# Expert gates built eight tokens at a time, on VectorE alone

## The chip, the cores and the metric

The kernel runs on one core of one Trainium2 chip. The metric is the device time of one execution in microseconds; lower is better. All times below are of that core.

## The reference, cut to what matters

A two-layer network over 256 latent tokens and 256 context tokens, 1024 features wide. Each layer has a mixer (gMLP in layer 0, S5 in layer 1) and then a PEER expert network: each token picks, in each of 8 heads, 16 of 128 x 128 = 16384 experts by a product of two keys, and adds up `gate * gelu(h . u) * v` over the 128 picked experts.

```python
s = einsum("nhkd,hkmd->nhkm", q, sub_keys)         # scores of both key halves
s_half, i_half = top_k(s, 16)
cand = s_half[:, :, 0, :, None] + s_half[:, :, 1, None, :]
top_s, top_c = top_k(cand.reshape(128, 8, 256), 16)
k1 = take(i_half[:, :, 0], top_c // 16); k2 = take(i_half[:, :, 1], top_c % 16)
ids = k1 * 128 + k2
g = softmax(top_s)
act = gelu(einsum("nd,nhkd->nhk", h, u_tab[ids]))
out = einsum("nhk,nhkd->nd", g * act, v_tab[ids])
```

## The kernel before

**Dense experts.** For the first 384 tokens of layer 0 and all 256 latents of layer 1 the kernel doesn't gather rows. It multiplies the tokens with all 16384 experts, in 128 chunks of 128 (`k1` is the chunk, `k2` the row in it), and weights each activation with a gate that is zero where the token didn't pick the expert. `dense` has two halves. In the first, `front(k1)` for the first chunks (62 of 64 in layer 0, 66 of 68 in layer 1, then the last two) loads 512 KB of `peer_ut`, splits it into a high and a low part (`uh` by ScalarE at L296, `ul` by VectorE and GpSimd in turn at L298: one of three by VectorE in layer 0, one of two in layer 1), multiplies on TensorE (24 products, L304 to L306), applies GELU (L708) and puts the result into DRAM. After each of these chunks `during(k1)` moves the other work of the stage on by an even share of its steps. In the second half `back(k1)` reads the gates back (`Gr`), weights the activations and multiplies with `peer_v`.

**The other work of the first half** is a chain written in `layer0` (L1351) and `layer1` (L1422): `route` of a block of 128 tokens (top-16 searches on VectorE), then the next block's `route` in turn with the first block's `gate_units`, and so on; the last block's `gate_units` runs alone. Layer 0 has three blocks, layer 1 two. `between()` drains this chain, and the last two `front`s are issued behind the last gate product (`issue_after(ends["gates"])`, L751), so the second half starts behind it.

**`gate_units`** (L626) builds the table `gd[group, k2, k1, token]`. Keys and gates of the block are transposed, so that the 128 picks lie on partitions and the tokens along the row. For four tokens (`R = 4`) it makes one-hot rows: `o2` marks the pick's `k2` (L664, VectorE), `eq` its `k1` (L666, VectorE); `o1` holds `eq` times the gate's high part (L668, VectorE) and low part (L669: GpSimd, but VectorE for the third block of layer 0). All are float16. `iot`, the numbers 0 to 127 each written four times, is made once at the start (L457). In the tiles the token is the innermost index, so the product of token m reads its operands at a step of four elements, 8 bytes:

```python
nc.tensor.matmul(o, o2[:, :, m], o1[:, 0, :, m], start=True, stop=False)
nc.tensor.matmul(o, o2[:, :, m], o1[:, 1, :, m], start=False, stop=True)
```

There are eight such products (L653, L654) for four tokens; ScalarE copies the sum out of the bank (L655), and every 16 tokens go to DRAM. The products lag two steps behind the one-hot rows (`pend`), and `o2`, `eq` and `o1` have four buffers each. Each block has 32 such units; layer 0 has 96, layer 1 has 64.

**Order.** The work is written in program order, and a planner then orders the instructions of each engine by its own estimate of when each can run. Each engine executes its own list in that order. Only TensorE's order in the second half of `dense` and in S5 is as written.

Of the kernel before, what the change touches and what calls it, by code (L numbers as in the profile page):

```python
# [107 lines left out]
HG = 0  # L108


@with_exitstack
def tile_hybrid(ctx: ExitStack, tc: tile.TileContext, I, out, stop=None):
# [11 lines left out]
    def urgent(n):  # L124
        """A context of instructions that go before others."""
        return tc.high_priority(n) if n else ExitStack()
# [46 lines left out]
    def scale_cols(i, f, nf):  # L173
        """Norm gain times (1 + scale), for the blocks f..f+nf if they are a scale's."""
        for a, n, s in ((A1, i, 8), (A2, 2 + i, 32)):
            if s <= f < s + 8:
                b = slice(f - s, f - s + nf)
                nc.vector.tensor_scalar(a[:, i, b], mod[:, i, f:f + nf, :], 1.0, None, op0=OP.add)
                nc.vector.tensor_tensor(a[:, i, b], a[:, i, b],
                                        ng[:, n, b].unsqueeze(2).to_broadcast([P, nf, 2]), op=OP.mult)  # L180

    def ada_pe(pa, f):
        """Shift, scale and gate of the first mixer on the tensor engine: rows, transposed to columns."""
# [22 lines left out]
    def ada_rows(pa, blocks, cB=None, e=nc.vector):  # L206
        """The other modulations as row products, a block of 128 features at a time, on engine e."""
# [29 lines left out]
    def rsqrt(v, r, y):  # L237
        """r = 1 / sqrt(v): a first value from the exponent's bits, refined by Newton steps."""
# [8 lines left out]
    def norm_add(pl, pm, b, t0, t1, e=nc.gpsimd):  # L247
        """Add block b's squares of the columns t0..t1: all but the last blocks' in a tile, then over the
        features, to the first columns of pm, with tokens on partitions."""
# [14 lines left out]
    def norm_end(pl, pm, n, r=None):  # L264
        """1 / sqrt(mean of squares + eps) on every partition; computed with tokens on partitions."""
# [26 lines left out]
    def split(hi, lo, src, dve=1, gps=1):  # L292
        """src (float32) as hi + lo, exactly, both in the format of one-pass products; the lower
        part by DVE and GpSimd in turn, in the given proportion."""
# [5 lines left out]
    def mm3(o, pairs):  # L300
        """o = sum over pairs of lhsT^T rhs, each operand (hi, lo); lo times lo is below float32's rounding."""
# [7 lines left out]
    def modulate(pl, r, i, a, sh, parts, keep=None):  # L309
        """The normalised, modulated columns of XT as hi + lo, for parts (c, t0, t1, hi, lo); r from column parts[0].t0."""  # L310
# [14 lines left out]
    def residual(src, i, b, gate, part, view=lambda x: x):  # L325
        """XT block b += gate * src (columns as in XT)."""
# [8 lines left out]
    def gmlp(gw, hh, hl, r, vpump, vdone, upump, mid, pump):  # L335
        """Adds the mixer's output to XT; r = the norm of the result's columns."""
# [4 lines left out]
        with ExitStack() as st:  # L341
# [42 lines left out]
            def spatial(h):  # L384
# [10 lines left out]
                # the parts take the places of values that are no longer needed  # L395
# [16 lines left out]
            # the norm's gain and shift pass through the spatial product: gain * product + (shift * row sums + b_s)  # L412
# [43 lines left out]
    iot = cp.tile([P, KEYS, 4], F16, name="iot")  # L456
    nc.vector.tensor_copy(iot, i128.unsqueeze(2).to_broadcast([P, KEYS, 4]))  # L457
# [8 lines left out]
    def route(pr, S, gates, ids, kk, big={}):  # L466
        """Gates, both halves' keys and expert ids [P, heads, TOPK] from the scores [P, heads, 2, KEYS]."""
# [46 lines left out]
    # The score of a key is h . (w_q . key): the products of w_q with the keys come first.  # L514
    wp_d = [[dr.tile([P, KB, 512], F32, name=f"wp{i}_{q}") for q in range(4)] for i in range(2)]

    def wprime_units(pw, i, nb, e):
        """wp_d[i][pair of heads][d, block, (head, half, key)]; each step makes the products of one (head, half).
        e: the second engine of the copies."""
# [29 lines left out]
    def score_weights(i, pw, lo=(1, 2)):  # L549
        """The weights of scores, head by head, as (hi, lo)."""  # L550
# [9 lines left out]
    def scores(weights, ahead, pieces, S, done=lambda q: None):  # L560
        """S[block][token, head, half, key] from the pieces (hi, lo) of 128 tokens; ahead = weights already made."""
# [9 lines left out]
    def add_back(i, acc, a0, m, p0=0):  # L571
        """XT columns a0..a0+m += gate * acc, acc of [token, feature] from row p0."""
# [9 lines left out]
    # Experts of a token one by one: their rows are gathered.  # L582
    def gather_units(pg, i, hn, gates, ids, nh, finish, step=2):
        """Rows of the experts ids[:, head, slot], for nh heads; yields after `step` gathers; finish(acc)."""
# [35 lines left out]
    # All experts for the first n tokens: U^T chunks, GELU, gates (zero where an expert was not chosen), V chunks.  # L620
# [5 lines left out]
    def gate_units(pg, i, gates, kk, nt, g0, second):  # L626
        """gd[group, k2, k1, token] = the sum of the gates of expert (k1, k2), for nt tokens of a block. A gate
        is the sum of two float16, scaled by a power of two; places in a row are one-hot."""
        R = 4
        tr = pg.tile([P, 3, P], F32, name="jT", bufs=1)  # L630
# [3 lines left out]
        nc.scalar.copy(tr.rearrange("p q n -> p (q n)"), pm[:, 0:3 * P])  # L634
        kt = pg.tile([P, 2, P], F16, name="kt16", bufs=1)
        nc.vector.tensor_copy(kt, tr[:, 0:2])
        gt = pg.tile([P, 2, P], F16, name="gt16", bufs=1)
        gs = pg.tile([P, P], F32, name="gs", bufs=1)
        nc.vector.tensor_scalar(gs, tr[:, 2], GSCALE, None, op0=OP.mult)
# [3 lines left out]
        sh = [P, KEYS, R]  # L643
        pend = []

        def products(u, o1, o2):
# [4 lines left out]
            for m in range(R):  # L651
                o = pm[:, m * P:(m + 1) * P]
                nc.tensor.matmul(o, o2[:, :, m], o1[:, 0, :, m], start=True, stop=False)  # L653
                ends["gates"] = nc.tensor.matmul(o, o2[:, :, m], o1[:, 1, :, m], start=False, stop=True).ins  # L654
# [6 lines left out]
        for u in range(nt // R):  # L661
            ns = slice(u * R, u * R + R)
            o2 = pg.tile(sh, F16, name="o2", bufs=4)
            nc.vector.tensor_tensor(o2, iot, kt[:, 1, ns].unsqueeze(1).to_broadcast(sh), op=OP.is_equal)  # L664
            eq = pg.tile(sh, F16, name="eq", bufs=4)
            nc.vector.tensor_tensor(eq, iot, kt[:, 0, ns].unsqueeze(1).to_broadcast(sh), op=OP.is_equal)  # L666
            o1 = pg.tile([P, 2] + sh[1:], F16, name="o1", bufs=4)
            one = nc.vector.tensor_tensor(o1[:, 0], eq, gt[:, 0, ns].unsqueeze(1).to_broadcast(sh), op=OP.mult)  # L668
            second.tensor_tensor(o1[:, 1], eq, gt[:, 1, ns].unsqueeze(1).to_broadcast(sh), op=OP.mult)  # L669
            ends["places"] = one.ins  # L670
            pend.append((u, o1, o2))
            if len(pend) > 2:
                products(*pend.pop(0))
            yield
# [5 lines left out]
    def dense(pd, back_pool, i, n, hh, hl, ahead, keep, abanks, vbanks, during, between, pump,  # L680
              dve=(0, 1), vdve=(1, 1), finish=None):
        """The products of the first n tokens with all experts. The first `ahead` chunks' activations come
        before between(), all but the last `keep` of them put into DRAM."""
# [4 lines left out]
        def gate_rows(blk, g0, g1):  # L688
            """The gates of kg chunks, groups of tokens g0..g1."""
# [111 lines left out]
    def s5_setup(pp, sm):  # L801
        """The S5 mixer's powers and input coefficients; partitions are (direction, state)."""
# [56 lines left out]
        # powers of a in the order of a chunk's places, the second direction running backward  # L859
# [12 lines left out]
    def phase_units(pw):  # L872
        """ph_d[group, k] = (rot[0] + i rot[1]) ** k, where rho (rot[0] + i rot[1]) = a^L; the skip's gains added
        to the kernels' diagonals."""
# [677 lines left out]
```

## Time and profile before

| | |
|---|---|
| runs | 3183.05, 3179.83, 3183.05 us; median 3183.05 |
| span of the profiled execution | 3178.6 us (its first to its last instruction; 4.45 us below the median of the runs) |
| TensorE busy, mean granted clock | 2783.3 us, 88%; 0.935 |
| VectorE busy | 2500.6 us, 79% |
| ScalarE busy | 1325.5 us, 42% |
| GpSimd busy | 1777.4 us, 56% |
| all DMA | 738.94 MB, 232 GB/s over the span |

A busy share is a mean over stages with different limits. A TensorE interval includes its way through the array, and following ones overlap, so TensorE's throughput is read from the distance between starts. The granted clock is a share of full speed.

### The profile page before, as it was taken

The page shows a single profiled execution, that of the slowest core. Times are in us where ns is not written, and L with a number is a line of the kernel's source. Part 1 is how long each engine was busy: PE and PEld are TensorE (multiplying, and loading weights), DVE is VectorE, ACT ScalarE, POOL GpSimd, SP SyncE. Part 2 cuts the span into 40 slices and gives each one's busy share as a digit, 9 for nine tenths or more (in the row PEclk, how much of TensorE's full clock was granted, in tenths as well). Part 3 has the DMA queues.
Part 4 walks back from the last instruction along what each step waited for, and adds up shares of the span by engine and source line. Part 5 has one row for each costly group of instructions (what it writes and reads, how often), then busy time and mean ns, then how long its engine had stood idle before and what let it go on. Part 6 is the DMA issues. An engine that isn't in the chain of part 4 may idle for free.

```text
span 3178.6 us, 46803 instructions
## 1 busy us (share of the span) xinstructions
PE 2783.3 (88%) x16231; PEld 2456.9 (77%) x16231; DVE 2500.6 (79%) x4335; ACT 1325.5 (42%) x2460; POOL 1777.4 (56%) x1228
## 2 busy tenths in 40 slices
PE   5789939888878888899999997988888789999998
PEld 1478839887867666688888875888888788889997
DVE  7992898999997887798999996764799986644444
ACT  3332343344436332333333322334344555555554
POOL 4581663566672444488888883135456655544443
PEclk8989969988988999999999998999899989999999
DMA  7548743545446878799999987998356668876663
GB/s 249 170 134 284 251 159 120 172 160 187 173 160 232 275 257 282 242 316 315 313 318 320 315 287 241 324 333 238 113 182 199 231 214 283 288 233 208 203 208 111
DMA packets 412534, 738.94 MB, mean 232 GB/s; under 512 B 41604, under 2 KB 270212, under 8 KB 407176
## 3 DMA queue, kind: packets, MB, share of 16 engines
q1 hardware_dynamic: 308192, 507.84, 48.2%
q0 software_dynamic: 36864, 134.23, 12.6%
q10 hardware_dynamic: 67240, 93.88, 8.3%
q8 instruction: 127, 2.08, 0.3%
q14 instruction: 111, 0.91, 0.1%
HBM read 633.07 MB, written 102.77 MB: 232 GB/s over the span
## 4 chain that ended last, share of the span: by engine, by line
PE 31%; DVE 13%; DMA 12%; issue 6%; POOL 4%; ACT 1%; SPq 1%; DVEq 0%; ACTq 0%; POOLq 0%
PE bk L744 5%; PE bk L745 5%; PE bk L743 5%; PE bk L306 4%; PE bk L304 4%; PE bk L305 4%; DMA vr<-peer_v 4%; POOL row L591 2%; DMA row<-peer_v,ids 2%; DMA wp<-wpo 1%; DVE ul L298 1%; POOL vl L298 1%; DVE o L668 1%; DVE acc L614 1%; DVE adasv L218 1%
## 5 line engine op out<-in xcount | busy, mean ns | idle before, releaser
L306 PE MATMUL bk<-hxh,ul 128*128 128x384 f32 (+1 forms) x2048 | 658.0, 322 | 36.4 <-DVE ul L298 23.5
L304 PE MATMUL bk<-hxh,uh 128*128 128x384 f32 (+1 forms) x2048 | 658.5, 322 | 13.3 <-ACT act L708 7.3
L305 PE MATMUL bk<-hxl,uh 128*128 128x384 f32 (+1 forms) x2048 | 651.9, 318 | 0.0
L298 POOL TENSOR_TENSOR vl<-vr,vh 128x512 fp32r<-128x512 f32 x256 | 360.7, 1413 | 456.4 <-ACT vh L296 452.8
L744 PE MATMUL bk<-vl,wh 128*128 128x512 f32 x1280 | 519.1, 406 | 59.7 <-POOL vl L298 41.7
L743 PE MATMUL bk<-vh,wh 128*128 128x512 f32 x1280 | 513.5, 401 | 30.9 <-ACT vh L296 20.4
L298 POOL TENSOR_TENSOR ul<-ur,uh 128x512 fp32r<-128x512 f32 x299 | 429.1, 1442 | 179.2 <-ACT uh L296 174.2
L296 ACT ACTIVATE vh<-vr 128x512 fp32r<-128x512 f32 x512 | 315.4, 623 | 500.4 <-DMA vr<-peer_v 362.1
L745 PE MATMUL bk<-vh,wl 128*128 128x512 f32 x1280 | 510.6, 399 | 0.0
L296 ACT ACTIVATE uh<-ur 128x512 fp32r<-128x512 f32 x512 | 314.5, 629 | 400.1 <-PE bk L305 217.8
L306 PEld LDWEIGHTS bk<-hxh,ul 128*128 128x128 f32 x2048 | 405.7, 198 | 42.7 <-DVE ul L298 28.2
L304 PEld LDWEIGHTS bk<-hxh,uh 128*128 128x128 f32 x2048 | 406.5, 198 | 20.8 <-ACT act L708 8.5
L305 PEld LDWEIGHTS bk<-hxl,uh 128*128 128x128 f32 x2048 | 405.4, 198 | 6.1 <-issue 0.9
L298 DVE TENSOR_TENSOR wl<-w,wh 128x384 fp32r<-128x384 f32 (+1 forms) x256 | 190.9, 746 | 239.4 <-ACT wh L296 239.2
L744 PEld LDWEIGHTS bk<-vl,wh 128*128 128x128 f32 x1280 | 247.9, 194 | 132.7 <-POOL vl L298 58.9
L743 PEld LDWEIGHTS bk<-vh,wh 128*128 128x128 f32 x1280 | 247.5, 193 | 86.3 <-ACT vh L296 26.0
L745 PEld LDWEIGHTS bk<-vh,wl 128*128 128x128 f32 x1280 | 247.7, 194 | 50.9
L298 DVE TENSOR_TENSOR vl<-vr,vh 128x512 fp32r<-128x512 f32 x256 | 204.1, 808 | 70.8 <-ACT vh L296 70.7
L614 DVE SCALAR_TENSOR_TENSOR acc<-row,wts,acc 128x1024 f32<-128x1024 f32 x127 | 211.5, 1665 | 24.9 <-DMA row<-peer_v,ids 23.6
L601 DVE SCALAR_TENSOR_TENSOR gscr<-row,hn 128x1024 f16<-128x1024 f32 x128 | 217.1, 1696 | 12.7 <-DMA row<-peer_u,ids 11.8
L298 DVE TENSOR_TENSOR ul<-ur,uh 128x512 fp32r<-128x512 f32 x213 | 192.3, 904 | 42.0 <-ACT uh L296 40.6
L653 PE MATMUL bk<-o,o 128*128 128x128 f16 x640 | 162.0, 296 | 70.1 <-DVE o L668 70.0
(344 smaller groups left out, 5753.0 us busy)
## 6 DMA issues: line engine op xcount, KB each, us to landing
ur<-peer_ut SPq DMA_DIRECT2D x256, 512.0 KB, 4.5
vr<-peer_v SPq DMA_DIRECT2D x256, 512.0 KB, 4.7
gd<-Gs ACTq DMA_DIRECT2D x40, 1024.0 KB, 4.1
wqT<-peer_w_q SPq DMA_DIRECT2D x64, 512.0 KB, 7.4
adatv<-ada_t SPq DMA_DIRECT2D x58, 512.0 KB, 5.6
Gr<-gd SPq DMA_DIRECT2D x120, 192.0 KB, 6.8
wp<-wpo ACTq DMA_DIRECT2D x32, 512.0 KB, 12.1
wpi<-wp SPq DMA_DIRECT2D x16, 1024.0 KB, 6.3
```

What stands on the lines that cost most here:

```text
L296: nc.scalar.activation(hi, src, AF.Copy)
L298: return e.tensor_tensor(lo, src, hi.bitcast(F32), op=OP.subtract)
L304: nc.tensor.matmul(o, ah, bh, start=(i == 0), stop=False)
L305: nc.tensor.matmul(o, ah, bl, start=False, stop=False)
L306: last = nc.tensor.matmul(o, al, bh, start=False, stop=(i == n - 1))
L591: tc.keep_in_program_order(nc.gpsimd.indirect_dma_start(out=r[:], out_offset=None, in_=I[f"peer_{table}{i}"], in_offset=bass.IndirectOffse ...
L601: nc.vector.scalar_tensor_tensor(scr, r, 1.0, hn, op0=OP.mult, op1=OP.mult, accum_out=dots[:, h, k:k + 1])
L614: nc.vector.scalar_tensor_tensor(acc, r, w, acc, op0=OP.mult, op1=OP.add)
L653: nc.tensor.matmul(o, o2[:, :, m], o1[:, 0, :, m], start=True, stop=False)
L743: nc.tensor.matmul(o, wh[:, js], vh, start=first, stop=False)
L744: nc.tensor.matmul(o, wh[:, js], vl, start=False, stop=False)
L745: nc.tensor.matmul(o, wl[:, js], vh, start=False, stop=last)
```

## The change

`gate_units` works on eight tokens (`GR = 8`) in two VectorE instructions in place of four for every four tokens:

- one comparison writes the places of both keys into `eq[P, 2, 128, 8]`, which takes the place of `o2` and `eq`;
- one product writes both parts of the gate into `o1[P, 2, 128, 8]`; nothing of it is on GpSimd any more;
- the 16 products for eight tokens still go four tokens to a bank; they now read their operands at a step of eight elements, 16 bytes;
- `eq` and `o1` have three buffers in layer 0 and two in layer 1, of eight tokens each, where there were four of four tokens;
- `iot` is twice as long and is made at the head of each layer's gate work (`places`), in that stage's pool;
- the transposed keys and gates go from the bank straight to `kt` and `gs` by two ScalarE instructions; the copy `jT` and two VectorE instructions (L636, L639) are gone.

The number of steps that the chain counts is the same. The rest of the diff removes comments.

```diff
-    iot = cp.tile([P, KEYS, 4], F16, name="iot")
-    nc.vector.tensor_copy(iot, i128.unsqueeze(2).to_broadcast([P, KEYS, 4]))
+    def places(pg):
+        iot = pg.tile([P, KEYS, GR], F16, name="iot", bufs=1)
+        nc.vector.tensor_copy(iot, i128.unsqueeze(2).to_broadcast([P, KEYS, GR]))
+        return iot
...
-    def gate_units(pg, i, gates, kk, nt, g0, second):
+    def gate_units(pg, iot, i, gates, kk, nt, g0):
...
-        tr = pg.tile([P, 3, P], F32, name="jT", bufs=1)
...
-        nc.scalar.copy(tr.rearrange("p q n -> p (q n)"), pm[:, 0:3 * P])
         kt = pg.tile([P, 2, P], F16, name="kt16", bufs=1)
-        nc.vector.tensor_copy(kt, tr[:, 0:2])
+        nc.scalar.copy(kt.rearrange("p q n -> p (q n)"), pm[:, 0:2 * P])
...
-        nc.vector.tensor_scalar(gs, tr[:, 2], GSCALE, None, op0=OP.mult)
+        nc.scalar.activation(gs, pm[:, 2 * P:3 * P], AF.Copy, scale=GSCALE)
...
-        sh = [P, KEYS, R]
+        sh = [P, 2, KEYS, GR]
...
-                nc.tensor.matmul(o, o2[:, :, m], o1[:, 0, :, m], start=True, stop=False)
-                ends["gates"] = nc.tensor.matmul(o, o2[:, :, m], o1[:, 1, :, m], start=False, stop=True).ins
+                k = u * R % GR + m
+                nc.tensor.matmul(o, eq[:, 1, :, k], o1[:, 0, :, k], start=True, stop=False)
+                ends["gates"] = nc.tensor.matmul(o, eq[:, 1, :, k], o1[:, 1, :, k], start=False, stop=True).ins
...
-        for u in range(nt // R):
-            ns = slice(u * R, u * R + R)
-            o2 = pg.tile(sh, F16, name="o2", bufs=4)
-            nc.vector.tensor_tensor(o2, iot, kt[:, 1, ns].unsqueeze(1).to_broadcast(sh), op=OP.is_equal)
-            eq = pg.tile(sh, F16, name="eq", bufs=4)
-            nc.vector.tensor_tensor(eq, iot, kt[:, 0, ns].unsqueeze(1).to_broadcast(sh), op=OP.is_equal)
-            o1 = pg.tile([P, 2] + sh[1:], F16, name="o1", bufs=4)
-            one = nc.vector.tensor_tensor(o1[:, 0], eq, gt[:, 0, ns].unsqueeze(1).to_broadcast(sh), op=OP.mult)
-            second.tensor_tensor(o1[:, 1], eq, gt[:, 1, ns].unsqueeze(1).to_broadcast(sh), op=OP.mult)
-            pend.append((u, o1, o2))
-            if len(pend) > 2:
-                products(*pend.pop(0))
-            yield
+        for v in range(nt // GR):
+            ns = slice(v * GR, (v + 1) * GR)
+            eq = pg.tile(sh, F16, name="eq", bufs=3 - i)
+            nc.vector.tensor_tensor(eq, iot.unsqueeze(1).to_broadcast(sh), kt[:, :, ns].unsqueeze(2).to_broadcast(sh), op=OP.is_equal)
+            o1 = pg.tile(sh, F16, name="o1", bufs=3 - i)
+            nc.vector.tensor_tensor(o1, eq[:, 0:1].to_broadcast(sh), gt[:, :, ns].unsqueeze(2).to_broadcast(sh), op=OP.mult)
+            pend += [(v * GR // R + q, o1, eq) for q in range(GR // R)]
+            for _ in range(GR // R):
+                if len(pend) > 2:
+                    products(*pend.pop(0))
+                yield
...
-            ga = [gate_units(pt, 0, gk[j][0], gk[j][1], P, j * P // GT, nc.vector if j == 2 else nc.gpsimd) for j in range(3)]
+            iot = places(pt)
+            ga = [gate_units(pt, iot, 0, gk[j][0], gk[j][1], P, j * P // GT) for j in range(3)]
...
-            ga = [gate_units(pt, 1, gk[j][0], gk[j][1], P, j * P // GT, nc.gpsimd) for j in range(2)]
+            iot = places(pt)
+            ga = [gate_units(pt, iot, 1, gk[j][0], gk[j][1], P, j * P // GT) for j in range(2)]
```

## Rows read from the trace of the kernel before

**Rows 1.** The page: span, and VectorE's busy tenths in 40 slices.
```profile
span 3178.6 us, 46803 instructions
...
DVE  7992898999997887798999996764799986644444
```

**Rows 2.** Stretches of the gate work: engines' busy us, clock, DMA share, GB/s.
```profile
680.00:960.00 280.00, 232.82 (x1358) 213.78 (x1356) 271.07 (x563) 125.60 (x178) 195.25 (x149) 0.89 0.50 173
960.00:1013.00 53.00, 48.09 (x355) 44.16 (x354) 46.30 (x133) 38.20 (x46) 7.78 (x5) 0.89 0.58 222
...
2360.00:2614.00 254.00, 212.21 (x1603) 201.44 (x1602) 242.03 (x389) 131.48 (x205) 161.75 (x114) 0.91 0.61 210
```

**Rows 3.** The chain of waits at the end of layer 0's gate work.
```profile
1009.68 0.35 DVE o L669
...
1013.88 0.42 PE bk L304
```

**Rows 4.** Who waited for whom, 680 to 1013 us: us, times, longest.
```profile
PE bk L653 <- DVE o L668: 47.9, 29, 6.5
...
DVE o L664 <- PE bk L654: 14.3, 7, 5.0
```

**Rows 5.** VectorE's groups, 679.5 to 959 us: busy, mean ns, idle before.
```profile
L664 DVE TENSOR_TENSOR o<-iot,kt 128x512 f16<-128x512 f16 x64 | 55.4, 866 | 8.2 <-PE bk L654 8.2
L668 DVE TENSOR_TENSOR o<-eq,gt 128x512 f16<-128x512 f16 x64 | 51.1, 806 | 0.0
L666 DVE TENSOR_TENSOR eq<-iot,kt 128x512 f16<-128x512 f16 x64 | 43.3, 681 | 0.3 <-POOL o L669 0.3
L298 DVE TENSOR_TENSOR ul<-ur,uh 128x512 fp32r<-128x512 f32 x24 | 24.5, 1023 | 0.0
```

**Rows 6.** GpSimd's costliest group, 679.5 to 959 us.
```profile
L669 POOL TENSOR_TENSOR o<-eq,gt 128x512 f16<-128x512 f16 x64 | 80.9, 1275 | 43.9 <-DVE eq L666 29.3 <-PE bk L654 6.7 <-DVE gt L641 6.3
```

**Rows 7.** Timeline, all engines, 858 to 862.5 us: start, us.
```profile
857.92 2.28 POOL L298 TENSOR_TENSOR ul<-ur,uh 128x512 fp32r<-128x512 f32 x1
...
858.98 1.51 DVE L664 TENSOR_TENSOR o<-iot,kt 128x512 f16<-128x512 f16 x1
```

**Rows 8.** Timeline of VectorE, 860 to 884 us: three in a row, undisturbed.
```profile
868.44 0.41 DVE L668 TENSOR_TENSOR o<-eq,gt 128x512 f16<-128x512 f16 x1
868.77 1.21 DVE L499 TENSOR_TENSOR oh<-pf,i 128x1024 f32<-128x1024 f32 x1
869.91 0.41 DVE L666 TENSOR_TENSOR eq<-iot,kt 128x512 f16<-128x512 f16 x1
```

**Rows 9.** VectorE's copy that makes `iot`.
```profile
L457 DVE CAST iot<-i x1: 960/960/960, 1.3 to 1.3; 128x512 f16<-128x512 f32 x1
```

**Rows 10.** VectorE's groups in layer 1, 2355 to 2614 us.
```profile
L668 DVE TENSOR_TENSOR o<-eq,gt 128x512 f16<-128x512 f16 x64 | 52.2, 820 | 0.0
L664 DVE TENSOR_TENSOR o<-iot,kt 128x512 f16<-128x512 f16 x64 | 48.6, 761 | 3.9 <-PE bk L654 3.9
L298 DVE TENSOR_TENSOR ul<-ur,uh 128x512 fp32r<-128x512 f32 x48 | 46.6, 970 | 1.9 <-ACT uh L296 1.9
L666 DVE TENSOR_TENSOR eq<-iot,kt 128x512 f16<-128x512 f16 x64 | 46.1, 732 | 1.2 <-POOL o L669 0.9
```

**Rows 11.** Tiles `o1`, `o2` in layer 1's stretch: PE, PEld, DVE, POOL busy.
```profile
2360.00:2614.00 254.00, 71.34 (x512) 53.93 (x512) 95.80 (x128) 81.86 (x64) 0.91 0.61 210
```

**Rows 12.** Who waited for whom, VectorE, 2360 to 2614 us.
```profile
DVE o L664 <- PE bk L654: 3.9, 3, 2.5
```

**Rows 13.** Timeline of TensorE, 860 to 872 us: a front product, then gate products.
```profile
866.74 0.34 PE L304 MATMUL bk<-hxh,uh 128*128 128x384 f32 x1
866.92 0.29 PE L654 MATMUL bk<-o,o 128*128 128x128 f16 x1
867.03 0.30 PE L653 MATMUL bk<-o,o 128*128 128x128 f16 x1
867.15 0.30 PE L654 MATMUL bk<-o,o 128*128 128x128 f16 x1
```

More of the change, by code (lines that the diff above doesn't have):

```diff
@@ L108 @@
 HG = 0
+GR = 8
 @with_exitstack
@@ L642, in gate_units, with products @@
         yield
-        sh = [P, KEYS, R]
+        sh = [P, 2, KEYS, GR]
         pend = []
-        def products(u, o1, o2):
+        def products(u, o1, eq):
             if u % (GT // R) == 0:
@@ L660, in gate_units @@
         Gs = [None]
-        for u in range(nt // R):
-            ns = slice(u * R, u * R + R)
-            o2 = pg.tile(sh, F16, name="o2", bufs=4)
-            nc.vector.tensor_tensor(o2, iot, kt[:, 1, ns].unsqueeze(1).to_broadcast(sh), op=OP.is_equal)
-            eq = pg.tile(sh, F16, name="eq", bufs=4)
-            nc.vector.tensor_tensor(eq, iot, kt[:, 0, ns].unsqueeze(1).to_broadcast(sh), op=OP.is_equal)
-            o1 = pg.tile([P, 2] + sh[1:], F16, name="o1", bufs=4)
-            one = nc.vector.tensor_tensor(o1[:, 0], eq, gt[:, 0, ns].unsqueeze(1).to_broadcast(sh), op=OP.mult)
-            second.tensor_tensor(o1[:, 1], eq, gt[:, 1, ns].unsqueeze(1).to_broadcast(sh), op=OP.mult)
-            ends["places"] = one.ins
-            pend.append((u, o1, o2))
-            if len(pend) > 2:
-                products(*pend.pop(0))
-            yield
+        for v in range(nt // GR):
[9 more added lines that the diff above has]
+                yield
         for x in pend:
```

## The prediction

> **What bounds the kernel now.** I read the page first. Over the span of 3178.6 us VectorE is busy 79%, but its row of 40 slices shows nine tenths or more in slices 9 to 12 and 30 to 32, which hold most of the gate work of the two layers [rows 1]. So I looked at these stretches by themselves. From 680 to 960 us (gates of layer 0's first two blocks) VectorE is busy 271.1 of 280 us, TensorE 232.8, GpSimd 195.3, and the DMA engines half [rows 2]. From 2360 to 2614 us (layer 1) VectorE has 242.0 of 254, TensorE 212.2. In both the granted clock of TensorE is 0.89 to 0.91 of full speed [rows 2], so part of the time it is at the lower of its two levels, though there is work in every stretch. What it waits for is named: 47.9 us for `o1` from VectorE [rows 4]. In the other direction VectorE waits 14.3 us for the gate products to free a buffer. Last, does the gate work set the end of the stage? The chain at the end of layer 0's gates goes from `o1` at 1009.7 us to the `front` product at 1013.9 us that was held behind the last gate product [rows 3]. So what shortens the gate work brings the second half of `dense` forward by as much, until TensorE itself is full. TensorE's idle time is the room: 47.2 + 4.9 = 52.1 us from 680 to 1013, 41.8 us in layer 1 [rows 2].
>
> **VectorE's own work.** Undisturbed, a 128x512 float16 step takes 0.33 us from start to start, and a 128x1024 float32 step 1.14 us [rows 8]. With a fixed part c and x for each float32 element, c + 1024x = 1.14. If float16 went at the same rate, c + 512x = 0.33 would make c negative; so it goes faster, and with two at a time c + 256x = 0.33, x = 1.055 ns, c = 0.06 us. A new instruction has 2048 float16 elements: 0.06 + 1024x = 1.14 us. The other bound is one element at a time, 2.22 us. I take 1.14, because both the old and the new operands are rows of float16 neighbours with one operand repeated; only the run is longer.
>
> Layer 0, blocks one and two: 64 units x 3 x 0.33 = 63.4 us become 32 x 2 x 1.14 = 73.0, +9.6. Third block (all four on VectorE): 32 x 4 x 0.33 = 42.2 become 36.5, -5.7. Layer 1: as the first, +9.6. So VectorE's bare work grows by 13.5 us.
>
> **What VectorE waits for inside its instructions.** In the first two blocks the three groups took 55.4 + 51.1 + 43.3 = 149.8 us [rows 5]; at 0.41 each [rows 8] 192 instructions would take 78.7. The 71.1 us above that are not idle time in the profile; they lie inside the durations. The timeline shows how: GpSimd runs `ul` from 857.92 to 860.20, VectorE's step starts at 858.98 and ends at 860.49, about 0.3 us behind GpSimd's end, after 1.51 us [rows 7]. VectorE stood behind GpSimd's instruction. GpSimd was busy 195.3 us here, and L669, which goes, is 80.9 of them, 41% [rows 2, 6].
>
> What is left of the 71.1 us? If every GpSimd instruction that stays costs what it cost, 59%: 42 us. If instead each VectorE instruction meets GpSimd as often as before, only now 64 instead of 192 times, 59% of a third: 14 us. I take the middle, 28: -43 us. The `ul` steps lose too: 24 x (1.02 - 0.67) = 8.5 us (0.67 is 512 elements by the formula, 0.60, plus the 0.08 by which a duration outlasts the next start [rows 8]); 41% of it is -3.5. Layer 1: 146.9 us for 192 [rows 10] are 68.2 above 78.7; L669 is 81.9 of 161.8 us [rows 2, 11], 51%. What stays lies between 49% (33 us) and a third of that (11): middle 22, -46. The 48 `ul`: 48 x (0.97 - 0.67) = 14.4, 51% is -7.
>
> **Small things.** `iot` cost 0.96 us once [rows 9] and is now twice as long and made twice: at most 2 x 1.9 - 1.0 = +2.8. The two VectorE conversions that move to ScalarE (busy 125.6 of 280 us [rows 2]) are worth less than 1 us a block; I count both together as nothing. Without ScalarE's idle time they would cost five times two short copies, a few us.
>
> VectorE's relief: layer 0 is 43 + 3.5 - 9.6 + 5.7 = 43 us (from 29 to 57 by the bounds of the waits), layer 1 is 46 + 7 - 9.6 = 43 (32 to 54).
>
> **What of it reaches the end.** TensorE has 52.1 and 41.8 us of idle time in these stretches, and it does not pack without gaps: its list mixes gate products with `front` products that wait for `ul`, and it is then late next. I let 65% of layer 0's relief through, -28 us, against none and all. In layer 1 the buffers are two of eight tokens. Group v can start only when both products of group v-2 are done, and by the written order these come directly before it. Before, a unit needed the products of four units back, and the wait was 3.9 us in all [rows 12]. Behind a VectorE instruction that waits for TensorE stand the next `ul`, and behind them the `front` products. I let 40% through, -17 us. Layer 0 gets more room than it had (six units' worth for four), so its 14.3 us [rows 4] should not grow.
>
> Sum, against the profiled execution: 3178.6 - 28 - 17 = 3133.6. The runs' median lies 4.45 above its span, so **3138 us**.
>
> **Step of the operands.** The gate products read every fourth float16 now, 8 bytes apart, and every eighth after the change, 16 bytes. Today a gate product of 128 columns starts every 0.11 to 0.12 us, and a `front` product of 384 contiguous columns holds its place for 0.18 us [rows 13]: 0.9 ns a column against 0.47. Something already costs the short strided product double, its own weight load or the step. A longer step can cost nothing (if the weight load sets the pace) or another doubling, +0.12 us for each of 768 products in layer 0 and 512 in layer 1, 92 and 61 us of TensorE time. The room pays for 52.1 / 768 = 0.07 and 41.8 / 512 = 0.08 us each; beyond that the change loses. I take nothing for the sum, since the trace shows no product at a longer step.
>
> The Trainium skill, page "Advanced Engine Details and Errata", section "Memory Cachelines", speaks against the change here: SBUF lines are 16 bytes, and at least two hits on a line are needed to hide its latency. Two of the old operand's elements share a line, and of the new one's none do. By that rule the products slow down (it gives no size), and with the doubling as the size the sum would be the first rival's; the rows above cannot show it either way.
>
> **The rivals.**
>
> - *TensorE becomes the bound through the step of 16 bytes (slower).* Doubled products add 92 - 52.1 = 40 and 61 - 41.8 = 19 us if the idle time were filled whole and the clock stayed: 3183 + 59 = 3242. A busy TensorE would win back the clock (0.9 to 1 of some 590 us, up to 59 us), which bounds it from below at about 3183. I name 3210. For it: already 0.9 ns a column. Against: a weight load may hide it. It decides from about 0.19 us a product. Chance 0.15.
> - *The two buffers of layer 1 become a wait.* If each of its 32 groups waits 1.2 us, half of the longest wait today, 2.5 us [rows 12], that is 38 us and eats nearly all of the 43: layer 1 gives 5, layer 0 28: 3150. If each waits the whole 2.5 us, 80, layer 1 loses 37 and the total is 3192. Chance 0.14, a third of it at or above the time before.
> - *Everything arrives.* TensorE packs well and its clock rises: 43 + 41.8: 3098. Chance 0.13.
> - *VectorE takes one element at a time.* Each of 160 instructions costs 1.08 us more, 173 us against a relief of 86: 3270. Against it: the old shape clearly runs faster than that. Chance 0.04.
> - *No gain is passed on,* because the planner puts the `front` work so that TensorE's list stays as long: 3177 to 3190. Chance 0.09.
>
> **How the numbers follow.** The forecast has 0.45, with its own range of 3115 to 3165. No change that a measurement of this kernel can tell is within 0.2%, 6.4 us. Faster: 0.45 + 0.13 + two thirds of 0.14 + a little of the last rival, 0.69. Same: 0.11, mostly the last rival and the lower end of the first. Slower: 0.15 + 0.04 and bits of the others, less what lands within 0.2%: 0.20. The range leaves out 0.07 below (the best case beyond 3095) and about 0.13 above (the first rival's upper half and the fourth): 3095 to 3205.
>
> **What would show it.** VectorE's `eq` and `o1` at about 1.2 us undisturbed, 80 of each; 2.2 would be the fourth rival. Their mean below 1.7 us in the stretches. No L669 on GpSimd, and its `ul` steps shorter. The last gate product near 985 us in place of 1010, and layer 1's a further 15 to 20 us earlier. Distance between gate products 0.12 us: 0.2 or more is the first rival, with TensorE over 95% busy and VectorE waiting for it. Long waits of `eq` for the products in layer 1 alone are the second. The stages behind (second halves, S5) should keep their lengths; if they move, the prediction is wrong for a reason that I don't see.

## The result, and the profile after

The changed kernel is slower: 3266.89 us in the median of four runs (3258.82 to 3271.57), against 3181.72 for the kernel before in the same comparison (3179.83 to 3183.05). The ratio is 1.0265, 95% interval [1.0249, 1.028]. Forecast were 3138 us and a range of 3095 to 3205, so both missed, and the sign too. It came out beyond the first rival, the step of 16 bytes, which named 3210 and had 3242 as its upper bound.

The page of the changed kernel: span, busy times, VectorE's tenths, and the two groups of gate products.

```profile
span 3269.8 us, 46222 instructions
...
PE 2931.1 (90%) x16231; PEld 2522.1 (77%) x16231; DVE 2379.6 (73%) x3974; ACT 1336.5 (41%) x2465; POOL 1604.7 (49%) x1100
...
DVE  7992998985856588799899986764898554654444
...
L658 PE MATMUL bk<-o,eq 128*128 128x128 f16 x640 | 266.0, 416 | 11.8 <-DVE o L671 11.8
L659 PE MATMUL bk<-o,eq 128*128 128x128 f16 x640 | 264.6, 413 | 0.0
```

VectorE and GpSimd did get their relief: VectorE has 121 us less than the 2500.6 of before, GpSimd 173 us less than 1777.4, and VectorE's nines in slices 9 to 12 [rows 1] are now 8, 5, 8, 5. TensorE has the same 16231 products and 148 us more of busy time. The next view has the two stretches of gate work, and three short ones within layer 0's.

```profile
680.00:1080.00 400.00, 381.81 (x1763) 310.69 (x1763) 256.29 (x500) 176.42 (x231) 120.51 (x89) 0.79 0.42 152
2360.00:2712.00 352.00, 334.61 (x2093) 289.58 (x2094) 257.83 (x444) 172.13 (x273) 126.12 (x77) 0.89 0.57 193
...
860.00:864.00 4.00, 3.79 (x18) 2.39 (x17) 4.00 (x3) 1.19 (x2) 2.87 (x3) 1.00 0.96 346
...
868.00:872.00 4.00, 4.00 (x19) 2.50 (x18) 3.77 (x6) 2.18 (x2) 0.00 (x0) 0.50 0.19 77
...
1010.00:1070.00 60.00, 52.63 (x225) 32.11 (x223) 29.32 (x25) 30.14 (x28) 0.00 (x0) 0.50 0.30 123
```

In layer 0 TensorE is busy 381.8 of 400 us and VectorE 256.3. Before, it was VectorE that was full [rows 2]. The granted clock of layer 0's stretch is 0.79, where it was 0.89; from 1010 to 1070 us, with little but gate products on TensorE, it is 0.50, the lower of the two levels (1.2 of 2.4 GHz). Over the whole span its mean went from 0.935 to 0.916.

Who waits for whom turned round. Before, TensorE waited 47.9 us for `o1` and VectorE 14.3 us for the products [rows 4]. After, VectorE's waits from 680 to 1060 us:

```profile
DVE eq L669 <- PE bk L659: 86.7, 37, 6.5
```

The tile's view of `eq` (shortest, median and longest in ns, start of the first and the last in us): a product in layer 0 and in both layers, and the comparison:

```profile
L659 PE MATMUL bk<-o,eq x384: 405/413/422, 697.3 to 1072.1; 128*128 128x128 f16 x192
...
L659 PE MATMUL bk<-o,eq x640: 405/413/435, 697.3 to 2710.4; 128*128 128x128 f16 x160
...
L669 DVE TENSOR_TENSOR eq<-iot,kt x80: 1195/1226/2656, 685.6 to 2697.4; 128x2048 f16<-128x2048 f16 x80
```

VectorE's new instruction lasts 1.226 us in the median, as worked out. Layer 0's last gate product starts at 1072.1 us in place of 1013.6, layer 1's at 2710.4 in place of 2613.5. So layer 0 loses 59 us, layer 1 another 38, and the span 91. TensorE's timeline shows why:

```profile
860.07 0.33 PE L305 MATMUL bk<-hxh,uh 128*128 128x384 f32 x1
860.24 0.33 PE L306 MATMUL bk<-hxl,uh 128*128 128x384 f32 x1
...
861.21 0.42 PE L659 MATMUL bk<-o,eq 128*128 128x128 f16 x1
861.45 0.42 PE L658 MATMUL bk<-o,eq 128*128 128x128 f16 x1
861.68 0.41 PE L659 MATMUL bk<-o,eq 128*128 128x128 f16 x1
...
870.11 0.41 PE L659 MATMUL bk<-o,eq 128*128 128x128 f16 x1
870.34 0.41 PE L658 MATMUL bk<-o,eq 128*128 128x128 f16 x1
```

A gate product now starts every 0.23 to 0.24 us, where it was 0.11 to 0.12 [rows 13]: longer than a `front` product with three times the columns (0.17). At 861 us the granted clock is at its upper level, at 870 at the lower, and the distance is the same. So the products are not slow because the clock fell.

### The profile page after: what moved, and what is told of

The parts are those of the page before. It is cut to its first block, busy times and chain, and to the rows that moved or that the text cites. A ratio compares the mean times of both kernels' runs of the same rounds, so it can differ in the third digit from the quotient of the medians.

```text
span 3269.8 us, 46222 instructions
## 1 busy us (share of the span) xinstructions
PE 2931.1 (90%) x16231; PEld 2522.1 (77%) x16231; DVE 2379.6 (73%) x3974; ACT 1336.5 (41%) x2465; POOL 1604.7 (49%) x1100
## 4 chain that ended last, share of the span: by engine, by line
PE 54%; DVE 20%; DMA 11%; issue 7%; POOL 4%; ACT 2%; SPq 1%; DVEq 0%; ACTq 0%; POOLq 0%
PE bk L307 8%; PE bk L305 8%; PE bk L306 8%; PE bk L746 6%; PE bk L747 5%; PE bk L745 5%; PE bk L658 5%; PE bk L659 5%; DMA vr<-peer_v 3%; DMA row<-peer_v,ids 3%; PE bk L549 2%; DVE adasv L219 2%; POOL row L596 1%; DMA row<-peer_u,ids 1%; POOL vl L299 1%
## 5 line engine op out<-in xcount | busy, mean ns | idle before, releaser
L305 PE MATMUL bk<-hxh,uh 128*128 128x384 f32 (+1 forms) x2048 | 666.4, 325 | 11.8 <-ACT act L710 6.6
L658 PE MATMUL bk<-o,eq 128*128 128x128 f16 x640 | 266.0, 416 | 11.8 <-DVE o L671 11.8
L659 PE MATMUL bk<-o,eq 128*128 128x128 f16 x640 | 264.6, 413 | 0.0
L660 ACT ACTIVATE Gs<-bk 128x512 f32<-128x512 f32 x160 | 172.0, 1076 | 170.1 <-PE bk L659 164.5
```

The lines of the kernel that those rows point to most:

```text
L305: nc.tensor.matmul(o, ah, bh, start=(i == 0), stop=False)
L658: nc.tensor.matmul(o, eq[:, 1, :, k], o1[:, 0, :, k], start=True, stop=False)
L659: ends["gates"] = nc.tensor.matmul(o, eq[:, 1, :, k], o1[:, 1, :, k], start=False, stop=True).ins
L660: nc.scalar.activation(Gs[0][:, :, n4:n4 + R].rearrange("p k n -> p n k"), pm.rearrange("p (n k) -> p n k", n=R), AF.Copy, scale=1.0 / GSCALE)
```

## The experiments

The theory after the result: the products are slow because they read their operands 16 bytes apart, and without that the change would be a gain. First rival: the step costs little, and what lost was the two buffers of layer 1. A second question is which of a product's two operands it is, the moving one or the weights.

**A step of 8 bytes, and one of 4, in the changed kernel.** The eight tokens are kept in runs of four (or two), so that there are still two VectorE instructions for eight tokens and as many buffers, but a product reads with a step of four (two) elements.

```diff
+GW = 4        # 2 in the other run
...
-        kt = pg.tile([P, 2, P], F16, name="kt16", bufs=1)
+        kt = pg.tile([P, P // GR, 2, GR], F16, name="kt16", bufs=1)
...
-        sh = [P, 2, KEYS, GR]
+        sh = [P, 2, GR // GW, KEYS, GW]
...
-                k = u * R % GR + m
-                nc.tensor.matmul(o, eq[:, 1, :, k], o1[:, 0, :, k], start=True, stop=False)
+                g, k = divmod(u * R % GR + m, GW)
+                nc.tensor.matmul(o, eq[:, 1, g, :, k], o1[:, 0, g, :, k], start=True, stop=False)
...
```

> The changed kernel with the tokens of a one-hot tile in runs of four in place of eight: [key, group of 4, 128, 4]. Still two VectorE instructions for eight tokens and the same buffers, but the products read at a step of 8 bytes again. Theory (the step of 16 bytes doubles the distance between gate products, 0.234 us for 0.119): distance back to 0.12 us, VectorE's waits for the products below 40 us in place of 155, time below the kernel before, 3110 to 3165 us. Rival (few large buffers, products bunched behind long VectorE instructions): VectorE still waits over 100 us for products, and the time stays above 3220 us.

> The same with runs of two tokens: the products read at a step of 4 bytes. If reading by the line sets the pace even at 8 bytes, the distance between gate products falls to 0.06 to 0.08 us at the upper clock, and the time is 10 to 40 us below the run with a step of 8 bytes. If the weight load or the array sets it there, the distance stays 0.12 us and the time is that of the run with 8 bytes. If VectorE pays for runs of two, its instructions take over 1.5 us and the time is above.

Measured, against 3181.34 us of the kernel before: 3096.82 with 8 bytes, ratio 0.9742 [0.9713, 0.9771], below the range that was expected; 3080.72 with 4 bytes, 0.9681 [0.9652, 0.971], the fastest kernel here. The step alone turns a loss of 85 us into a gain of 85 us. The run with 8 bytes: products in a row, and the tile's view of them in layer 0 and in layer 1; the stretch; its two groups of gate instructions in layer 0; and VectorE's wait in layer 1:

```profile
850.00 0.30 PE L660 MATMUL bk<-o,eq 128*128 128x128 f16 x1
850.12 0.30 PE L661 MATMUL bk<-o,eq 128*128 128x128 f16 x1
850.24 0.30 PE L660 MATMUL bk<-o,eq 128*128 128x128 f16 x1
```

```profile
L661 PE MATMUL bk<-o,eq x384: 293/298/302, 687.9 to 963.1; 128*128 128x128 f16 x192
...
L661 PE MATMUL bk<-o,eq x256: 284/298/303, 2317.7 to 2526.0; 128*128 128x128 f16 x128
```

```profile
680.00:960.00 280.00, 256.85 (x1668) 246.98 (x1667) 268.61 (x473) 159.78 (x219) 140.00 (x86) 0.93 0.57 202
```

```profile
L675 DVE TENSOR_TENSOR o<-eq,gt 128x2048 f16<-128x2048 f16 x48 | 70.8, 1494 | 0.0
L673 DVE TENSOR_TENSOR eq<-iot,kt 128x2048 f16<-128x2048 f16 x48 | 63.3, 1331 | 3.3 <-PE bk L661 2.8 <-ACT kt L640 0.4
```

```profile
DVE eq L673 <- PE bk L661: 8.5, 10, 2.7
```

The distance is 0.12 us again. VectorE waits 2.8 us for products in layer 0 and 8.5 in layer 1, with the same three and two buffers: that rival falls. In the run with 4 bytes the distance halves once more:

```profile
850.89 0.22 PE L660 MATMUL bk<-o,eq 128*128 128x128 f16 x1
850.95 0.22 PE L661 MATMUL bk<-o,eq 128*128 128x128 f16 x1
851.01 0.22 PE L660 MATMUL bk<-o,eq 128*128 128x128 f16 x1
```

I averaged such distances over both layers' stretches by the granted clock. At 4 bytes it is 0.060 us at the upper level and 0.103 at the lower; at 8 bytes 0.118 at both; at 16 bytes 0.235 and 0.234. A `front` product of layer 0, 384 columns, has medians of 0.173 and 0.320 us in the same stretches. So at 4 bytes a column takes about what a contiguous one takes, and changes with the clock as that does.

**Which operand: the step of 16 bytes for one alone.** In the kernel before, in layer 0 only, `o1` (moving) or `o2` (weights) is spread over a tile twice as long; nothing else changes.

```diff
-            o1 = pg.tile([P, 2] + sh[1:], F16, name="o1", bufs=4)
+            o1 = pg.tile([P, 2, KEYS, R if i else 2 * R], F16, name="o1", bufs=4)[:, :, :, 0:R]
```
```diff
-            o2 = pg.tile(sh, F16, name="o2", bufs=4)
+            o2 = pg.tile([P, KEYS, R if i else 2 * R], F16, name="o2", bufs=4)[:, :, 0:R]
```

> The kernel before, with o1, the moving operand, in tiles twice as wide of which every second run of four is unused, in layer 0 only: a step of 16 bytes for the moving operand, 8 bytes for the weights. VectorE and GpSimd do the same instructions as before. If the moving operand is what is read slowly: distance 0.23 us in layer 0 and 0.12 in layer 1, time 3210 to 3250 us. If not: 0.12 in both, time within 10 us of before.

> The kernel before, with o2, the weights, at a step of 16 bytes in layer 0 only, the moving operand at 8. If the weight load is what is read slowly: distance 0.2 us or more in layer 0, weight loads longer than the 117 ns of before, time 3210 to 3250 us. If not: 0.12 us and a time within 10 us of before.

Measured: moving operand 3217.86, ratio 1.0116 [1.0078, 1.0153]; weights 3184.76, 1.0012 [0.9992, 1.0031]. Products by tile in the first of these, layer 0 and then layer 1, whose step is still 8 bytes; and its stretch in layer 0:

```profile
L653 PE MATMUL bk<-o,o x384: 387/410/433, 686.2 to 1049.6; 128*128 128x128 f16 x192
...
L653 PE MATMUL bk<-o,o x256: 278/297/330, 2404.9 to 2648.8; 128*128 128x128 f16 x128
```

```profile
680.00:1060.00 380.00, 376.23 (x1761) 287.52 (x1759) 318.02 (x702) 176.30 (x230) 209.77 (x157) 0.85 0.47 164
```

The weight load in the kernel before, and then the weights' run, layer 0:

```profile
L653 PEld LDWEIGHTS <-o x640: 110/117/151, 686.7 to 2613.3; 128*128 128x128 f16 x160
```

```profile
L653 PEld LDWEIGHTS <-o x384: 142/146/173, 688.6 to 1016.1; 128*128 128x128 f16 x192
L653 PE MATMUL bk<-o,o x384: 276/303/345, 688.6 to 1016.2; 128*128 128x128 f16 x192
```

It is the moving operand. The weight load grows from 117 to 146 ns too, but a product still starts every 0.12 to 0.13 us. With the moving operand alone the last gate product of layer 0 comes 36 us later than before, and the kernel takes 36.5 us more: near the first rival's 92 - 52.1 = 40 us for layer 0. The clock of the stretch falls from 0.89 to 0.85 while TensorE is busy 99% of it; the rival's lower bound had it rise.

**What the rest of the change gains, part by part.** The 85 us of the run with 8 bytes are about twice the 45 of the forecast. Three runs take it apart: the kernel before with L669 on VectorE in all blocks; the two-instruction form with four tokens at a time and a step of 8 bytes; and the kernel before with a step of 4 bytes alone. The first and the third edit are against the kernel before, the second against the version with 8 bytes; of each only the line that matters is shown (the first stands in layer 1 too, `o1` has the buffers of `eq`).

```diff
-            ga = [gate_units(pt, 0, gk[j][0], gk[j][1], P, j * P // GT, nc.vector if j == 2 else nc.gpsimd) for j in range(3)]
+            ga = [gate_units(pt, 0, gk[j][0], gk[j][1], P, j * P // GT, nc.vector) for j in range(3)]
```
```diff
-GR = 8
+GR = 4
...
-            eq = pg.tile(sh, F16, name="eq", bufs=3 - i)
+            eq = pg.tile(sh, F16, name="eq", bufs=2 * (3 - i))
...
```
```diff
...
-        sh = [P, KEYS, R]
+        sh = [P, 2, KEYS, 2]
...
```

> The kernel before with only one part of the change: the gate's low part on VectorE in all blocks (four short instructions for four tokens, none on GpSimd). Theory (VectorE is the bound; it pays 0.33 us of its own for each instruction and stands behind GpSimd at some of them): 128 instructions more are 42 us, and 41 to 51% of the waits of 139 us go, but 256 in place of 192 instructions can meet what stays, so 55 to 70 us of it remain in each layer or less: the sum is within 25 us of before, 3160 to 3205 us. Rival (taking GpSimd out is the whole gain of the run with 8 bytes): 3085 to 3125 us.

> The run with a step of 8 bytes, but four tokens at a time: the same two kinds of VectorE instruction on 1024 elements, 320 of them in place of 160, buffers doubled in number so that they hold as many tokens. VectorE's own work grows by 160 times 0.06 us, 10 us. Theory (each VectorE instruction that starts while GpSimd reads waits for it, so half as many instructions wait half as often): 20 to 50 us slower than the run with eight at a time, 3115 to 3150 us. Rival (the number of instructions doesn't matter, only that GpSimd has less): 3095 to 3110 us.

> The kernel before with its tokens in runs of two, so that the gate products read at a step of 4 bytes; the same four instructions on VectorE and GpSimd. The distance between gate products should be 0.06 us. Theory (VectorE, not TensorE, was the bound before): at most 20 us faster, 3160 to 3185 us. Rival (most of the gain of the run with 4 bytes is TensorE's): 3090 to 3140 us.

Measured against 3184.5: L669 on VectorE 3123.78, ratio 0.9806 [0.9783, 0.983]; two instructions for four tokens 3095.29, 0.9728 [0.9703, 0.9752]; step 4 bytes alone 3177.66, 0.9978 [0.9967, 0.9989]. So taking L669 off GpSimd is most of it, 61 us, far more than the theory expected and within the rival's range, though VectorE gets 128 more instructions by it. Joining the instructions, together with the conversions that move to ScalarE, gives another 28; the two were not tried apart. Eight tokens at a time in place of four gives nothing: 0.9728 and 0.9742 are the same. In the traces 320 gate instructions have 46 us in all above their undisturbed 0.68 us, and 160 have 35 above 1.22, while VectorE's `ul` steps are 10 us shorter with 320. So the waits grow far less than the number of instructions. And faster products gain only 7 us where VectorE is the bound.

VectorE's gate groups with L669 on VectorE, 679 to 955 us:

```profile
L666 DVE TENSOR_TENSOR eq<-iot,kt 128x512 f16<-128x512 f16 x79 | 45.6, 605 | 0.0
L669 DVE TENSOR_TENSOR o<-eq,gt 128x512 f16<-128x512 f16 x76 | 37.3, 500 | 0.0
L664 DVE TENSOR_TENSOR o<-iot,kt 128x512 f16<-128x512 f16 x77 | 37.2, 493 | 0.0
L668 DVE TENSOR_TENSOR o<-eq,gt 128x512 f16<-128x512 f16 x76 | 36.3, 484 | 0.0
```

Their sum is 156.4 us for 308 instructions; at 0.41 each that is 126.3 and 0.10 us above it per instruction. In the kernel before it was 0.37 [rows 5].

**Is it GpSimd's work, or the dependence on it?** L669 could have cost VectorE time because GpSimd was busy, or because it is released by VectorE's `eq` and so always started together with VectorE's next step. Two runs give GpSimd a spare multiply of L669's shape back, 64 times in layer 0, into a tile that nobody reads; one reads `iot`, the other `eq`.

```diff
-            second.tensor_tensor(o1[:, 1], eq, gt[:, 1, ns].unsqueeze(1).to_broadcast(sh), op=OP.mult)
+            nc.vector.tensor_tensor(o1[:, 1], eq, gt[:, 1, ns].unsqueeze(1).to_broadcast(sh), op=OP.mult)
+            if i == 0 and second is nc.gpsimd:
+                xx = pg.tile(sh, F16, name="xx", bufs=1)
+                nc.gpsimd.tensor_tensor(xx, iot, gt[:, 1, ns].unsqueeze(1).to_broadcast(sh), op=OP.mult)  # other run: eq
```

> The kernel before with L669 on VectorE in all blocks (as the earlier run with everything on VectorE, 3123.8 us), and in layer 0's first two blocks GpSimd gets back a multiply of the same shape as L669 for each four tokens, into a tile that nobody reads; it reads iot and gt, so it waits for no step of VectorE. Layer 0's gate instructions of VectorE had 0.10 us above their undisturbed 0.41 in that earlier run, against 0.37 in the kernel before. Theory (what cost VectorE was GpSimd's busy time, whatever it depends on): the excess goes back towards 0.25 to 0.37 us for some 256 instructions, 40 to 70 us of VectorE, of which most reaches the end: 3150 to 3190. Rival (what cost was the dependence: a GpSimd step that is released by VectorE's step and so starts together with the next one): little is left of it here, 3122 to 3138.

> The same as the run beside it, but GpSimd's spare multiply reads eq and gt, as L669 did, so that it is released by VectorE's comparison; still nobody waits for its result, except that eq's buffer comes free later. Both theories expect the excess of VectorE's instructions to come back, 3150 to 3190: then this run and the one beside it tell the two apart only by their distance, near 0 by the theory of GpSimd's busy time, 20 us or more by the rival of the dependence. If both stay at 3122 to 3138, GpSimd's work was not the cost at all, and it was VectorE's or TensorE's waiting for L669's late result that the kernel with everything on VectorE got rid of.

Measured against 3181.26: 3185.9 with `iot`, ratio 1.0017 [1.0005, 1.0028]; 3170.21 with `eq`, 0.997 [0.9954, 0.9985]. The run that reads `iot`:

```profile
L669 DVE TENSOR_TENSOR o<-eq,gt 128x512 f16<-128x512 f16 x64 | 51.3, 809 | 0.0
L668 DVE TENSOR_TENSOR o<-eq,gt 128x512 f16<-128x512 f16 x64 | 47.2, 743 | 0.0
L664 DVE TENSOR_TENSOR o<-iot,kt 128x512 f16<-128x512 f16 x64 | 44.2, 701 | 0.0
L666 DVE TENSOR_TENSOR eq<-iot,kt 128x512 f16<-128x512 f16 x64 | 39.6, 635 | 0.0
...
L672 POOL TENSOR_TENSOR xx<-iot,gt 128x512 f16<-128x512 f16 x62 | 77.4, 1249 | 7.0 <-DVE gt L641 5.4
```

```profile
L654 PE MATMUL bk<-o,o x384: 274/297/330, 689.9 to 1025.3; 128*128 128x128 f16 x192
```

The 256 instructions take 182.3 us, 0.30 above 0.41 each: most of the waits are back, from work that nobody needs and that waits for no step of VectorE. Layer 0's last gate product moves from 982.0 us to 1025.3, and to 1029.6 where the spare multiply reads `eq`. The dependence adds 4 us there; it is not the cause, and that rival falls. The run with `iot` is nevertheless 15 us slower as a whole. From layer 0's last gate product to layer 1's first it takes 1372 us, where the other run, the kernel with L669 on VectorE and the kernel before take 1354 to 1356. Most of that arises in the S5 mixer, which has no spare multiply in either run; why is not shown.

**More of `ul` on GpSimd.** On top of the version with 4 bytes, VectorE does one `ul` for every four of GpSimd's in layer 0, in place of one for two, and one for two in layer 1, in place of one for one.

```diff
-                      during, between, back_work, DV0, VV0)
+                      during, between, back_work, (1, 4), VV0)
...
-                dense(pd, lambda: pd, 1, n, hh, hl, AHEAD1, 8, (0, 1), (4, 5, 6, 7), during, between, back_work1, DV1, VV1, finish)
+                dense(pd, lambda: pd, 1, n, hh, hl, AHEAD1, 8, (0, 1), (4, 5, 6, 7), during, between, back_work1, (1, 2), VV1, finish)
```

> The run with a step of 4 bytes, with fewer of the chunks' low parts (ul) on VectorE in the first half: one of five in place of one of three in layer 0, one of three in place of one of two in layer 1; the others on GpSimd. If VectorE is still the bound there (94% busy in layer 0's stretch), some 12 steps of 0.9 us each in layer 0 and as many in layer 1 come back: 3055 to 3075 us. If GpSimd's longer steps (1.7 us) are late next, or make VectorE wait more often: 3080 us or more.

Measured: 3105.12, 0.9755 [0.9733, 0.9778], so 24 us slower than the version with 4 bytes. GpSimd's `ul` in layer 0 in that version, then here, with VectorE's comparisons beside it:

```profile
L300 POOL TENSOR_TENSOR ul<-ur,uh 128x512 fp32r<-128x512 f32 x53 | 91.5, 1733 | 79.2 <-ACT uh L298 77.4 <-PE bk L308 1.6
```

```profile
L300 POOL TENSOR_TENSOR ul<-ur,uh 128x512 fp32r<-128x512 f32 x67 | 140.9, 2117 | 76.0 <-ACT uh L298 76.0
...
L673 DVE TENSOR_TENSOR eq<-iot,kt 128x2048 f16<-128x2048 f16 x44 | 69.3, 1598 | 0.1
```

VectorE has 17 `ul` here, against 27 in the version it is built on, and GpSimd's went from 1733 to 2117 ns each. The 44 comparisons against 48 in these 276 us are no sign of longer waits: the first starts 6.6 us later (685.1 against 678.5), and their mean is about the same (1598 and 1576 ns). The last gate product comes 12 us later in layer 0 and 20 in layer 1. So the work taken off VectorE did not bring the gates' end forward, and GpSimd's steps got longer by it; what cost the 24 us is not shown.

## Why the prediction was wrong

**The step that failed: "I take nothing for the sum"** for the step of the operands. It cost all that the text had as its other bound. The rival's term was 0.12 us for each of 1280 products, 92 + 61 us; measured are 0.234 - 0.118 = 0.116 us, 89 and 59. The reason given, that the trace shows no product at a longer step, spoke for neither end. The one pair of rows that sets a strided product against a contiguous one showed a doubling, 0.9 against 0.47 ns a column [rows 13]. The weight load, 117 ns long, explained it as well, so that the trace before couldn't decide; but nothing in it spoke for zero more than for another doubling. The middle, 0.06 us a product, would have taken 46 and 31 of TensorE's 52.1 and 41.8 us of idle time, and left room for 17 us of gain at most. The runs show which it was: 0.47, 0.92 and 1.83 ns a column at 4, 8 and 16 bytes, which is 1.83 to 1.88 ns for every 16 bytes that the moving operand spans. The two longer steps alone show this as the cost of the read, since at 4 bytes the distance follows the clock.

The Trainium skill, "Advanced Engine Details and Errata", section "Memory Cachelines", spoke against the change, and its direction was right. Its measure of two hits on a line is not: at 8 bytes two elements share a line of 16, and the product is still twice as slow as at 4 (0.118 against 0.060 us). Here the measurement decides.

**The first rival was still too kind.** Its 40 + 19 us took TensorE's idle time as filled; 18 us of it stay in layer 0's stretch. Its lower bound, that a busy TensorE wins back clock, was wrong in sign. What the whole change costs against its own version with 8 bytes is 3266.9 - 3096.8 = 170 us: 1280 x 0.116 = 149 for the products themselves. The rest is about what the lower clock takes from the `front` products between them. In the two stretches 195 + 227 of these have the lower level and start 0.326 and 0.220 us apart, against 0.178 and 0.127 at the upper one (means, without distances over 0.6 us), so 29 + 21 us; the same sum for the version with 8 bytes is 5 + 4. That makes 149 + 41 = 190, where the spans of the two traces that it is read from differ by 186 (3269.8 and 3083.9). That the slow reads lower the clock is what these two traces and the run with the spread `o1` have in common; it was not tried apart from the length of the stretch.

**VectorE's own work was right:** 1.226 us measured against 1.14 and the 0.08 by which a duration outlasts the next start.

**The waits behind GpSimd were sized well enough, their mechanism was half right.** For layer 0 the forecast left 28 of 71.1 us. The version with 8 bytes has 134.1 us for 96 instructions in layer 0, 17 above 1.22 each; layer 1 has 17.6 above 64 x 1.22, forecast 22. The lower bound, that each instruction meets GpSimd as often as before, fell: by it twice as many instructions would wait twice as long, and they had 46 us in place of 35. The `ul` steps, from which the forecast took 3.5 and 7 us, wait more and not less: 15.7 us above 0.67 each in layer 0's stretch, where it was 8.5, and 23 in layer 1's, where it was 14. That GpSimd's work is what VectorE waits behind held, in the run with the spare multiply. But L669 was 41% of GpSimd's busy time and carried about two thirds of the waits: 77.3 us above 0.41 with the spare multiply (256 instructions), 25 of them without (30.1 x 64 / 77 groups).

The Trainium skill has a rule for such waits, in "SBUF - State Buffer", section "SBUF: two separate sides": VectorE and GpSimd share one pair of ports, which one instruction holds from start to end, and a VectorE instruction with two inputs in SBUF and a GpSimd instruction that reads SBUF shut each other out. The traces agree as far as they show it: a GpSimd multiply of 1.25 us that nobody needs costs the gates' end 43 us in 64, or 0.68 us each.

**What reaches the end was too low.** The forecast let 65% and 40% through, 28 + 17 us. In the version with 8 bytes layer 0's last gate product comes 50 us earlier than before and layer 1's a further 37, of VectorE relief of some 54 - 4 = 50 and 51 - 10 = 41 us without the `ul` steps. VectorE's busy time in the two stretches fell by 48 and 43 us. Nearly all arrives, and that version's 3096.8 us stand where the third rival, everything arrives, had 3098. Two buffers in layer 1 are enough: the second rival fell with the wait of 8.5 us. The fourth (one element at a time) fell with the 1.226 us, so that its 3270 lies near the measured time by chance; the last (no gain passed on) with the 50 and 37.

So the forecast missed by two terms of opposite sign: it had 170 us too little for the cost of the step, and 40 too little for the gain of the rest.

## What to carry to other kernels

When tokens are packed innermost so that VectorE gets longer instructions, look at the step at which TensorE then reads its moving operand, and cost it by the nearest rows: nothing forces the wide tile and the long step together, and runs of two tokens in a tile of eight keep both gains (3080.7 us, against 3181.3 before and 3266.9 after). When an engine's full row holds waits inside its instructions, the sum of durations above the undisturbed one is worth more than the busy share: taking an instruction from GpSimd onto the full VectorE made the kernel 61 us faster. And where a trace leaves a cost between nothing and a doubling, don't take nothing for the sum; take the row it is nearest to.

## What the runs showed of the hardware that was not expected

- A float16 product of 128 columns starts every 0.060, 0.118 and 0.234 us with its moving operand at a step of 4, 8 and 16 bytes. The last two are the same at both levels of the clock; only the first changes with it (0.103 at the lower).
- A step of 16 bytes in place of 8 in the weights adds 29 ns to a weight load and nothing that a measurement can tell to the kernel (1.0012 [0.9992, 1.0031]).
- A TensorE busy 99% of a stretch, with slowly read products, had a lower granted clock there than the one before, busy 84%: 0.85 against 0.89. In the changed kernel's 60 us with little but such products it had 0.50.
- A multiply on GpSimd that nothing waits for, 64 times in one stage, moved the end of that stage's gate work back by 43 us. The kernel became 62 us slower, and 16 of these arose later, where there is no spare multiply.
